# Slot dependences by quarter, a separate conversion clock, second V buffers and a halo prefetch in a hybrid decoder layer

## Chip, cores, metric

One Trainium2 chip, all 8 cores. Each core computes half of one of four sequences (2048 own tokens; the second half also needs keys and values of the first). The metric is the device time of the slowest core in microseconds. Most executions agree within 0.3%; in some, the cores of one die show a lower granted clock (TensorE's clock as the profile gives it, as a share of the full one) and the time is some per cent longer ("slow state").

## The reference, cut to what matters

```python
h = rmsnorm(x, norm_mix_pre)                       # x: (4, 4096, 2048)
q, k, v, u, g_attn, g_pool = split(h @ w_in)       # 1024, 1024, 1024, 1024, 2048, 2048
y_attn = stick_breaking_attention(q, k, v) @ w_attn_branch   # 8 heads of 128
y_pool = (pool(u) grouped @ w_pool_group * pool_scale) @ w_pool_branch
x = x + rmsnorm((sigmoid(g_attn)*y_attn + sigmoid(g_pool)*y_pool) @ w_out)
h = rmsnorm(x); up = causal_conv3(h @ w_up)        # 2 * 5632
x = x + rmsnorm((gelu(gate) * val) @ w_down)
x = x + rmsnorm(sigmoid(x @ w_ple_gate) * (p @ w_ple))
```

Stick-breaking weights telescope, so the kernel multiplies differences of neighbouring V rows: every V row is needed once more, shifted by one row.

## The kernel before

The program is recorded in Python: `P.op` and `P.dma` compare the regions that an instruction reads and writes with earlier ones and add semaphore waits. Timers (`after`) place later steps at a model time `now`, which advances with the recorded matmuls. A hold on a region fires timers early when a new instruction would collide with it (`guard`).

A core handles 8 chunks of 512 tokens: K and V for all, Q for the last four. From chunk 5 on this is interleaved on TensorE with attention(0), whose first part computes two halo tokens (extra tokens that the later three-tap convolution needs besides the core's own). Then come four mixers (U and pooling, gates, output projection), the first three beside attention(1) to (3), then the feed-forward and embedding parts. Weights come through eight slots of 512 KB. Mixer weights are first converted from float32 to bf16, DRAM to DRAM, two units at a time, by GpSimd's DMA queue.

```python
def mmq(pieces, reads, writes, start=True, q=4):       # 16 matmuls in quarters
    for a in range(0, n, q):
        ...
        P.op("pe", f, reads=reads, writes=writes)
        yield ...
# a token-major group (V of chunks 5..7, U, output projection): 4 slots, 4 blocks of tokens
rd = [s[1].r() for s in sl]                            # every quarter reads all four slots
for q_, ns in enumerate(mmq(pieces, rd + [hT[hb].r()], [bkr(b)])):
    if streamed and blk == 3:
        W.done(sl[q_][0])                              # frees the slot: refilled at once
    yield ns

def conv_every(ns):
    if conv:
        convert(conv[0], conv[0] + 2); conv.popleft()  # 1 MB written, 2 MB read
        after(ns, lambda: conv_every(ns))              # re-arms at now + ns

def t1():                                              # end of p0_v(c): the shifted V
    P.dma("sp", s_v[0], [(Vs[0:127], Vv[1:128]), (Vs[127:128, :, 0:3, :], Vv[0:1, :, 1:4, :]),
                         (Vs[127:128, :, 3, :], upv[0:1])], ...)
...
after(2000, t1, ...); after(11000, t2, ...)            # t2: subtraction on DVE
after(16500, t3, ...)                                  # t3: store of the differences

for h in range(NH):                                    # halo tokens in attention(0)
    kb_ = ldk(cc, h)                                   # load, used by the very next matmul
    P.op("pe", ... kb_ ...)
    yield 1500, 213
```

Of the kernel before, what the change touches and what calls it, by code (L numbers as in the profile page):

```python
# [216 lines left out]
def build_program():  # L217
# [23 lines left out]
    with contextlib.ExitStack() as es:  # L241
# [85 lines left out]
        off[0] = mix_lo  # L327
        wk = alloc(16 * 1024, BF16)
        assert off[0] <= mix_hi
        Vb = Buf(SBT, oT[1].lo, 4096, BF16)  # L330
        Vsh = Buf(SBT, G[1].lo, 4096, BF16)

        def bfm(i, j):
            return Buf(SBT, (hT[i % 2].lo, hT[i % 2].lo + 8192, oT[i % 2].lo, sga.lo)[j], D, F32)
# [11 lines left out]
        def bkr(b, n=1):  # L346
            return ("ps", b, b + n)
# [96 lines left out]

        def drain_all():
            drain()
            while timers:
                fire()

        def chain(entries, bufs=()):  # L450
# [5 lines left out]
        def dma_after(ns, q, sem, pairs, reads, writes):  # L456
            after(ns, lambda: P.dma(q, sem, pairs, reads=reads, writes=writes), reads, writes)

        def mmq(pieces, reads, writes, start=True, q=4):
            n = len(pieces)  # L460
            for a in range(0, n, q):
                sub = pieces[a:a + q]

                def f(e, sub=sub, a=a):
                    ins = None
                    for i, (o, l, r) in enumerate(sub):
                        ins = e.matmul(o, l, r, start=(start and a + i == 0), stop=(a + i == n - 1), skip_group_check=True)  # L467
                    return ins
                P.op("pe", f, reads=reads, writes=writes)
                yield sum(p[2].shape[-1] for p in sub) / 2.4  # L470

        def mm_now(pieces, reads, writes, start=True):
# [62 lines left out]
            P.dma("pool", s_cv, [(ws[u0:u1].rearrange("n p c -> (n p) c"), wst[u0:u1].rearrange("n p c -> (n p) c"))],  # L535
                  writes=[("ws", u0, u1)])

        def conv_every(ns):
            if conv:
                convert(conv[0], conv[0] + 2)  # L540
                conv.popleft()
                after(ns, lambda: conv_every(ns))

        def conv_all(u):
            while conv and conv[0] <= u:
# [136 lines left out]
                    yield ns  # L682
                kq_out(b, KS[c, h], ("ks", c * 8 + h, c * 8 + h + 1))

        Vv = Vb.v().rearrange("p (h b d) -> p h b d", h=NH, b=4)
        Vs = Vsh.v().rearrange("p (h b d) -> p h b d", h=NH, b=4)
        upv = uprev.v().rearrange("p (h d) -> p h d", d=128)

        def p0_v(c, streamed):
            hb = c % 2  # L690
            hv = hTv[hb]
            for cg in range(2):
                if streamed:
                    sl = [W.take(U_V + cg * 4 + ku) for ku in range(4)]
                for blk in range(4):
                    b = nb()
                    if streamed:
                        pieces = [(bank(b), hv[:, k, blk * 128:(blk + 1) * 128], sl[k // 4][1].k3(512)[:, k % 4, :]) for k in range(16)]
                        rd = [s[1].r() for s in sl]
                    else:  # L700
                        pieces = [(bank(b), hv[:, k, blk * 128:(blk + 1) * 128], wv3[:, cg * 16 + k, :]) for k in range(16)]
                        rd = [wv.r(cg * 8192, (cg + 1) * 8192)]
                    for q_, ns in enumerate(mmq(pieces, rd + [hT[hb].r()], [bkr(b)])):
                        if streamed and blk == 3:
                            W.done(sl[q_][0])
                        yield ns
                    evac(Vv[:, cg * 4:cg * 4 + 4, blk, :], bank(b).rearrange("p (h d) -> p h d", d=128), [bkr(b)], [Vb.r()])
            vr, vsr_, ur = Vb.r(), Vsh.r(), uprev.r()
            dvreg = ("dvs", c * 8, c * 8 + 8)

            def t1():
                P.dma("sp", s_v[0], [(Vs[0:127], Vv[1:128]), (Vs[127:128, :, 0:3, :], Vv[0:1, :, 1:4, :]),
                                     (Vs[127:128, :, 3, :], upv[0:1])], reads=[vr, ur], writes=[vsr_])
                if c >= 3:
                    P.dma("sp", s_v[2], [(VS[c - 3].rearrange("h p x -> p h x"), Vb.v().rearrange("p (h x) -> p h x", h=NH))],
                          reads=[vr], writes=[("vs", c - 3, c - 2)])

            def t2():
                for hh in range(2):
                    P.op("dve", lambda e, hh=hh: e.tensor_tensor(  # L720
                        out=Vsh.v(hh * 2048, (hh + 1) * 2048), in0=Vsh.v(hh * 2048, (hh + 1) * 2048),
                        in1=Vb.v(hh * 2048, (hh + 1) * 2048), op=ALU.subtract), reads=[vsr_, vr], writes=[vsr_])

            def t3():
                P.dma("sp", s_v[3], [(DVS[c].rearrange("h p x -> p h x"), Vsh.v().rearrange("p (h x) -> p h x", h=NH))],
                      reads=[vsr_], writes=[dvreg])
                P.dma("sp", s_v[1], [(upv[0:1], Vv[0:1, :, 0, :])], reads=[vr], writes=[ur])
            vsd = [("vs", c - 3, c - 2)] if c >= 3 else []
            after(2000, t1, [vr, ur], [vsr_] + vsd)
            after(11000, t2, [vr], [vsr_])  # L730
            after(16500, t3, [vr], [vsr_, ur, dvreg])
# [21 lines left out]
        def attention(t, pos0=0):  # L753
# [21 lines left out]
            if t == 0:  # L775
                yield 20000, 0
                prev = None
                for cc in range(3, -1, -1):
                    b = ZB[zb[0] % 2]
                    zb[0] += 1  # L780
                    for h in range(NH):
                        kb_ = ldk(cc, h)
                        P.op("pe", lambda e, kb_=kb_, h=h, b=b: e.matmul(bank(b), qh.v(h * 128, (h + 1) * 128), kb_.v(), start=(h == 0),
                                                                     stop=(h == 7), skip_group_check=True),
                             reads=[kb_.r(), qh.r()], writes=[bkr(b)])
                        yield 1500, 213
                    gb = gr.next()
                    P.op("act", lambda e, gb=gb, b=b: e.activation(out=gb.v(), in_=bank(b), func=AF.Sigmoid, scale=-QSCALE),
                         reads=[bkr(b)], writes=[gb.r()])
# [18 lines left out]
                    evac(asb.v(), at[:, 0:NT], [bkr(ab)], [asb.r()], eng="act")  # L808
                    yield 2000, 0
                    for h in range(NH):  # L810
                        dv = lddv(cc, h)
                        rd = [dv.r(), asb.r()]
                        pcs = [(bank(OB, 2, 2 * h), dv.v(kb * 128, (kb + 1) * 128), asb.v(kb * 128 + 2 * h, kb * 128 + 2 * h + 2))
                               for kb in range(4)]
                        if cc == 3:
                            vv = ldv(3, h)
                            pcs.append((bank(OB, 2, 2 * h), vv.v(0, 128), idz.v(0, 2)))
                            rd += [vv.r(), idz.r()]

                        def f(e, pcs=pcs, first=(cc == 3 and h == 0)):  # L820
                            ins = None
                            for i, (o_, l, r) in enumerate(pcs):
                                ins = e.matmul(o_, l, r, start=(first and i == 0), stop=False, skip_group_check=True)
                            return ins
                        P.op("pe", f, reads=rd, writes=[bkr(OB)])
                        yield 1500, 250
                evac(o.k3(NTH)[:, :, NT:NTH], bank(OB, 16).rearrange("p (h t) -> p h t", t=2), [bkr(OB)], [o.r()], eng="dve")

            groups = [(h, cc) for h in range(NH) for cc in range(c, -1, -1)]
# [127 lines left out]
        def att_total(t):  # L957
            c = 4 + t
            n = NH * (c * 4 * 640 + (10 * 128 * 3 + 512) / 2.4) + 4000
            if t == 0:  # L960
                n += 20000 + 4 * (8 * 1500 + 7000 + 8 * 1500)
            return n

        def mixer(i):
            hb = i % 2
# [2 lines left out]
            pcs_cols = [(0, 257), (257, 514)] if i == 0 else [(0, 512)]  # L968
            wcol = NTH if i == 0 else NT

            def load_h(j):
                P.dma("sp", s_hT[j % 2], [(hTv[j % 2][:, :, 0:NT], H1[j].rearrange("p (k t) -> p k t", t=NT))],
                      reads=[("h1", j, j + 1)], writes=[hT[j % 2].r()])
            if i == 0:
                load_h(0)
                ctx = Buf(SBT, XN[0].lo, 2048, BF16)
                P.dma("sp", s_st[2], [(ctx.v(), HC)], reads=[("hc", 0, 1)], writes=[ctx.r()])
                P.op("dve", lambda e: e.tensor_copy(hv[:, :, NT:NTH], h2c.v().rearrange("p (k t) -> p k t", t=2)),
                     reads=[h2c.r()], writes=[hT[hb].r()])
            for cg in range(2):  # L980
                sl = [W.take(U_U + cg * 4 + ku) for ku in range(4)]
                for blk in ([4] if i == 0 else []) + [0, 1, 2, 3]:
                    b = nb()
                    if blk == 4:
                        lhs = lambda k: ctx.k3(128)[:, k, :]
# [4 lines left out]
                        rd = [hT[hb].r()]  # L990
                        dst, dr = ub.v(blk * 1024 + cg * 512, blk * 1024 + cg * 512 + 512), ub.r(blk * 1024, (blk + 1) * 1024)
                    pieces = [(bank(b), lhs(k), sl[k // 4][1].k3(512)[:, k % 4, :]) for k in range(16)]
                    for q_, ns in enumerate(mmq(pieces, rd + [s[1].r() for s in sl], [bkr(b)])):
                        if blk == 3:
                            W.done(sl[q_][0])
                        yield ns
# [85 lines left out]
            for cg in range(4):  # L1082
                sl = [W.take(U_O + cg * 4 + ku) for ku in range(4)]
                blks = [0, 1, 2, 3] + ([4] if i == 0 else [])
                for blk in blks:
# [3 lines left out]
                    ob = bank(b) if blk < 4 else PS[0:2, b * 512:b * 512 + 512]  # L1089
                    pieces = [(ob, mxT.v(k * NTH + c0, k * NTH + c0 + m), sl[k // 4][1].k3(512)[:, k % 4, :]) for k in range(16)]  # L1090
                    lastb = blk == blks[-1]
                    for q_, ns in enumerate(mmq(pieces, [s[1].r() for s in sl] + [mxT.r()], [bkr(b)])):
                        if lastb:
                            W.done(sl[q_][0])
                        yield ns
# [113 lines left out]
        front(1)  # L1209
        run(p0_k(0))  # L1210
        drain()
        conv_every(11500)
        run(p0_k(1))
        run(p0_v(0, False))
        front(2)
# [13 lines left out]
        def p0b():  # L1229
            for c in range(5, 8):  # L1230
                drain()
                p0_begin(c)
                if c < 7:
                    front(c + 1)
                for x_ in phase(p0_k(c), p0_v(c, True), p0_q(c)):
                    yield x_
        stats.append(run(p0b(), attention(0), 72 * GRP, att_total(0)))
# [445 lines left out]
```

## Time and profile before

| | us |
|---|---|
| median of 20 runs (lowest, highest) | 5706.8 (5692.4, 6051.1) |
| profiled run, slowest core | 5689.3 |
| first work of the feed-forward part | 3494.5 |
| PE busy, share of the span | 4498.0, 79% |

The slices show where to look: each digit is PE's busy share, or the granted clock, of a fortieth of the span, in tenths.

```profile
PE   5201676458679978977997786999999999999988
...
PEclk9655888679889989988998897999999999999999
```

The second to fourth slices are the hole; slices 5 to 11 are the chunks and the halo tokens; the dips at 15, 18 and 19, 22 and 23, and 25 are output projections; from slice 26 on PE is full. Two more lines belong to each chunk's shift. The first is from the timeline of the SyncE queue (start, duration of the issues), the second from the chain that ended last.

```profile
674.84 19.74 SPq L202 DMA_DIRECT2D SB<-SB  x3
```

```profile
693.30 24.43 DMA SB<-SB
```

Issuing the shift's three transfers holds the SyncE queue 20 us, and the data lands 24 us later. All else that SyncE loads stands behind it: the next issue in the timeline is at 694.73 us. From 706 to 716 us only its packets move: 32 of 8 KB, one after another, 0.31 us each, 26 GB/s and 6.3% of the 16 DMA engines' time.

The same trace shows what the clock costs. In the first output projection, at a clock of 0.83, the three groups of four matmuls between refill waits that the prediction prints took 1.02, 1.86 and 1.87 us: the second and third 0.84 and 0.85 us longer than the first, besides the waits themselves.

### The profile page before, as it was taken

The numbers are of one execution on the slowest core, as the hardware profiler recorded it, in microseconds if no ns is written. First come the engines' busy times: TensorE is split into PE (matmuls) and PEld (weight loads), VectorE is DVE, ScalarE is ACT, GpSimd is POOL, SyncE is SP. The second block draws the span as 40 slices with busy tenths as digits, with TensorE's granted clock in tenths as the row PEclk, the third lists the DMA queues.
The fourth block names the chain that finished last, engine by engine and source line by source line (L and its number), as shares of the span: only waits on it lengthen the run. The fifth ranks groups of instructions, "written<-read, shape, count | busy, mean of one in ns | idle before, by whom it ended". The sixth has DMA issues, their size and how long they took to land.

```text
span 5689.3 us, 73576 instructions; the slowest of 8 cores (5664.5 to 5689.3 us)
## 1 busy us (share of the span) xinstructions
PE 4498.0 (79%) x25664; PEld 2331.5 (41%) x25664; DVE 2278.7 (40%) x2149; ACT 1846.1 (32%) x3066; POOL 284.5 (5%) x652
## 2 busy tenths in 40 slices
PE   5201676458679978977997786999999999999988
PEld 2000332124348534533553333666644444444434
DVE  2000221017547647855884313444411444431154
ACT  2000111016445536644663212333300233320134
POOL 1000000000000000000000001111100111100000
PEclk9655888679889989988998897999999999999999
DMA  9898244334334334434443436777756644446653
GB/s 192 101 113 114 87 140 134 107 100 126 111 124 139 124 106 155 140 109 139 148 141 114 161 126 132 139 127 128 127 173 212 152 78 77 76 107 198 200 204 113
DMA packets 292013, 752.95 MB, mean 132 GB/s; under 512 B 61386, under 2 KB 174474, under 8 KB 270602
## 3 DMA queue, kind: packets, MB, share of 16 engines
q1 hardware_dynamic: 259156, 566.54, 30.3%
q0 software_dynamic: 32496, 181.72, 21.6%
q8 instruction: 213, 3.49, 0.3%
q14 instruction: 148, 1.21, 0.1%
HBM read 827.59 MB, written 171.44 MB: 176 GB/s over the span
## 4 chain that ended last, share of the span: by engine, by line
PE 69%; DMA 14%; another core or an unknown queue 7%; SPq 4%; DVE 3%; issue 2%; ACT 1%; POOL 0%; DVEq 0%; ACTq 0%; POOLq 0%
PE PS L467 30%; PE PS L1302 20%; PE PS L1353 9%; DMA SB<-ws 5%; SPq L202 4%; PE PS L914 3%; PE PS L881 3%; PE PS L843 3%; DMA SB<-SB 1%; DMA KS<-SB 1%; DMA SB<-KS 1%; DMA SB<-X 1%; DMA SB<-DVS 1%; DMA SB<-xr 1%
## 5 line engine op out<-in xcount | busy, mean ns | idle before, releaser
L467 PE MATMUL PS<-SB 128*128 128x512 bf16 (+2 forms) x9656 | 2141.0, 370 | 399.8 <-DMA SB<-ws 264.3
L467 PEld LDWEIGHTS PS<-SB 128*128 128x128 bf16 x9656 | 905.5, 100 | 1268.0 <-issue 576.0
L1302 PE MATMUL PS<-SB 128*128 128x342 bf16 (+1 forms) x7040 | 1228.5, 337 | 7.3 <-ACT SB L1319 7.3
L486 ACT ACTIVATE SB<-PS 128x512 bf16<-128x512 bf16 (+4 forms) x1017 | 608.7, 604 | 1716.7 <-PE PS L881 475.3
L771 DVE TENSOR_TENSOR_SCAN SB<-SB 128x512 bf16<-128x512 f32 (+1 forms) x836 | 975.4, 1201 | 217.4 <-ACT SB L854 187.4
L1302 PEld LDWEIGHTS PS<-SB 128*128 128x128 bf16 x7040 | 683.0, 97 | 551.9 <-issue 11.8
L1353 PE MATMUL PS<-SB 128*128 128x512 bf16 x2816 | 613.4, 381 | 12.6 <-DMA SB<-ws 12.5
L568 ACT ACTIVATE SB<-SB 128x512 bf16<-128x512 f32 (+3 forms) x245 | 216.7, 885 | 968.8 <-DVE SB L490 785.8
L490 DVE COPY SB<-PS 128x512 f32<-128x512 f32 (+3 forms) x197 | 135.2, 687 | 965.4 <-PE PS L1353 441.0
L589 PE MATMUL PS<-SB 128*128 128x128 bf16 x1024 | 81.2, 243 | 549.9 <-DVE SB L574 530.7
L854 ACT ACTIVATE SB<-PS 128x512 f32<-128x512 f32 (+1 forms) x832 | 476.6, 573 | 34.5 <-PE PS L843 19.0
L1326 DVE SCALAR_TENSOR_TENSOR SB<-SB 128x1024 f32<-128x1024 f32 x176 | 226.1, 1285 | 614.9 <-ACT SB L1319 614.9
L1353 PEld LDWEIGHTS PS<-SB 128*128 128x128 bf16 x2816 | 275.9, 98 | 348.0 <-issue 20.3
L1316 ACT ACTIVATE SB<-PS 128x1026 f32<-128x1026 f32 (+1 forms) x176 | 180.2, 1024 | 686.9 <-PE PS L1302 675.8
L914 PE MATMUL PS<-SB 128*128 128x512 bf16 (+1 forms) x960 | 322.4, 358 | 40.7 <-DMA SB<-DVS 35.6
L490 DVE CAST SB<-PS 128x512 bf16<-128x512 f32 (+2 forms) x151 | 97.9, 652 | 611.4 <-PE PS L467 404.0
L881 PEld LDWEIGHTS PS<-SB 128*128 128x128 bf16 x3136 | 249.9, 100 | 187.4 <-issue 28.8
L843 PE MATMUL PS<-SB 128*128 128x512 bf16 (+1 forms) x832 | 313.2, 377 | 14.7 <-ACT SB L854 12.9
L881 PE MATMUL PS<-SB 128*128 128x128 bf16 x3136 | 321.6, 224 | 2.3 <-ACT SB L486 1.1
L589 PEld LDWEIGHTS PS<-SB 128*128 128x128 bf16 x1024 | 73.6, 110 | 567.9 <-issue 557.7
L574 DVE SCALAR_TENSOR_TENSOR SB<-SB 128x2048 f32<-128x2048 f32 (+2 forms) x98 | 229.8, 2345 | 116.3 <-POOL SB L563 100.0
L1329 DVE SCALAR_TENSOR_TENSOR SB<-SB 128x1024 f32<-128x1024 f32 x176 | 226.1, 1285 | 18.4
(53 smaller groups left out, 1460.7 us busy)
## 6 DMA issues: line engine op xcount, KB each, us to landing
SB<-ws SPq DMA_DIRECT2D x520, 512.0 KB, 3.5
SB<-wst POOLq DMA_DIRECT2D x192, 512.0 KB, 6.2
ws<-wst POOLq DMA_DIRECT2D x74, 1024.0 KB, 42.0
SB<-xr SPq DMA_DIRECT2D x48, 1024.0 KB, 7.9
SB<-X SPq DMA_DIRECT2D x36, 1024.0 KB, 9.1
X<-SB SPq DMA_DIRECT2D x32, 1024.0 KB, 7.3
SB<-KS SPq DMA_DIRECT2D x240, 128.0 KB, 2.8
SB<-DVS SPq DMA_DIRECT2D x240, 128.0 KB, 3.0
```

The costliest lines, as they stand in the source:

```text
L202: e.dma_start(out=o, in_=i).then_inc(h, 16)
L467: ins = e.matmul(o, l, r, start=(start and a + i == 0), stop=(a + i == n - 1), skip_group_check=True)
L486: P.op("act", lambda e: e.activation(out=dst, in_=src, func=AF.Copy), reads=reads, writes=writes)
L490: P.op("dve", lambda e: e.tensor_copy(dst, src), reads=reads, writes=writes)
L574: P.op("dve", lambda e: e.scalar_tensor_tensor(out=dst, in0=xv, scalar=cv, in1=gv, op0=ALU.mult, op1=ALU.mult), reads=[xr_, small.r(col, c ...
L771: P.op("dve", lambda e: e.tensor_tensor_scan(out=pb.v(lo, NT), data0=gb.v(lo, NT), data1=mask, initial=init, op0=ALU.mult, op1=ALU.max), r ...
L843: P.op("pe", lambda e: e.matmul(bank(bk, NT - lo, lo), q_.v(b_ * 128, (b_ + 1) * 128), kb_.v(lo, NT), start=True, stop=True), reads=[kb_.r ...
L854: P.op("act", lambda e: e.activation(out=gb.v(lo, NT), in_=bank(bk, NT - lo, lo), func=AF.Sigmoid, scale=-QSCALE), reads=[bkr(bk)], writes ...
L881: ins = e.transpose(at[:, q_ * 128:(q_ + 1) * 128], src[q_].v(kb * 128, (kb + 1) * 128), ident)
L914: ins = e.matmul(o_, l, r, start=(first and i == 0), stop=False, skip_group_check=True)
L1302: ins = e.matmul(bank(bs[bi], c1 - c0), w3[:, k, :], hT2v[:, k, c0:c1], start=(k == 0), stop=(k == 15), skip_group_check=True)
L1353: ins = e.matmul(bank(b), actb[kk].v(q_ * 512 + blk * 128, q_ * 512 + (blk + 1) * 128), w3[:, k, :], start=(kk == 0), stop=(kk == NF - 1), ...
```

## The change

Intent: remove waits of TensorE before the feed-forward part by (1) letting each quarter of a token-major group depend on its own slot, (2) re-arming the conversion timer from its own scheduled time, 13 us apart, and not draining it with the other timers, (3) giving chunk 1's V buffers of its own in weight slots not yet in use, (4) loading halo keys and values two ahead, (5) loading the first mixer's inputs during chunk 7. The diff, cut to its core:

```diff
-            while timers:
+            while any(t[2] is not None for t in timers):
                 fire()
...
-        def mmq(pieces, reads, writes, start=True, q=4):
+        def mmq(pieces, reads, writes, start=True, q=4, rq=None):
...
-                P.op("pe", f, reads=reads, writes=writes)
+                P.op("pe", f, reads=reads + ([rq[a // q]] if rq else []), writes=writes)
...
-        def conv_every(ns):
+        def conv_every(ns, t=None):
+            t = now[0] if t is None else t
             if conv:
                 convert(conv[0], conv[0] + 2)
                 conv.popleft()
-                after(ns, lambda: conv_every(ns))
+                after(t + ns - now[0], lambda: conv_every(ns, t + ns))
...
+            Vb, Vsh = (Vb0, Vsh0) if c != 1 else (Buf(SBT, ringb[0].lo, 4096, BF16), Buf(SBT, ringb[2].lo, 4096, BF16))
...
+                for _ in range(2):
+                    more_k()
+                    more_v()
...
-                        kb_ = ldk(cc, h)
+                        kb_ = kl.popleft()
                         P.op("pe", ...)
-                        yield 1500, 213
+                        more_k()
+                        yield 2000, 213
... (the same for differences and values)
-                    for q_, ns in enumerate(mmq(pieces, [s[1].r() for s in sl] + [mxT.r()], [bkr(b)])):
+                    for q_, ns in enumerate(mmq(pieces, [mxT.r()], [bkr(b)], rq=[s[1].r() for s in sl])):
... (the same for V and U; in U the halo block moves from first to fourth)
-        conv_every(11500)
+        conv_every(13000)
...
+                else:
+                    mixer_first_loads()
```

More of the change, by code (lines that the diff above doesn't have):

```diff
@@ L329, in build_program @@
         assert off[0] <= mix_hi
-        Vb = Buf(SBT, oT[1].lo, 4096, BF16)
-        Vsh = Buf(SBT, G[1].lo, 4096, BF16)
+        Vb0 = Buf(SBT, oT[1].lo, 4096, BF16)
+        Vsh0 = Buf(SBT, G[1].lo, 4096, BF16)
         def bfm(i, j):
@@ L683, in p0_k @@
                 kq_out(b, KS[c, h], ("ks", c * 8 + h, c * 8 + h + 1))
-        Vv = Vb.v().rearrange("p (h b d) -> p h b d", h=NH, b=4)
-        Vs = Vsh.v().rearrange("p (h b d) -> p h b d", h=NH, b=4)
         upv = uprev.v().rearrange("p (h d) -> p h d", d=128)
@@ L690, in p0_v @@
             hb = c % 2
+            Vb, Vsh = (Vb0, Vsh0) if c != 1 else (Buf(SBT, ringb[0].lo, 4096, BF16), Buf(SBT, ringb[2].lo, 4096, BF16))
+            Vv = Vb.v().rearrange("p (h b d) -> p h b d", h=NH, b=4)
+            Vs = Vsh.v().rearrange("p (h b d) -> p h b d", h=NH, b=4)
             hv = hTv[hb]
@@ L698, in p0_v @@
                         pieces = [(bank(b), hv[:, k, blk * 128:(blk + 1) * 128], sl[k // 4][1].k3(512)[:, k % 4, :]) for k in range(16)]
-                        rd = [s[1].r() for s in sl]
+                        rd = []
                     else:
@@ L702, in p0_v @@
                         rd = [wv.r(cg * 8192, (cg + 1) * 8192)]
-                    for q_, ns in enumerate(mmq(pieces, rd + [hT[hb].r()], [bkr(b)])):
+                    for q_, ns in enumerate(mmq(pieces, rd + [hT[hb].r()], [bkr(b)], rq=[s[1].r() for s in sl] if streamed else None)):
                         if streamed and blk == 3:
@@ L777, in attention, with more_k, more_v @@
                 prev = None
+                kq = deque((cc, h) for cc in range(3, -1, -1) for h in range(NH))
+                vq = deque(kq)
+                kl, vl, sl_ = deque(), deque(), deque()
+                def more_k():
+                    if kq:
+                        kl.append(ldk(*kq.popleft()))
+                def more_v():
+                    if vq:
+                        cc_, h_ = vq.popleft()
+                        if cc_ == 3:
+                            sl_.append(ldv(3, h_))
+                        vl.append(lddv(cc_, h_))
+                for _ in range(2):
+                    more_k()
+                    more_v()
+                yield 4000, 0
                 for cc in range(3, -1, -1):
@@ L810, in attention @@
                     for h in range(NH):
-                        dv = lddv(cc, h)
+                        dv = vl.popleft()
                         rd = [dv.r(), asb.r()]
@@ L815, in attention @@
                         if cc == 3:
-                            vv = ldv(3, h)
+                            vv = sl_.popleft()
                             pcs.append((bank(OB, 2, 2 * h), vv.v(0, 128), idz.v(0, 2)))
@@ L825, in attention @@
                         P.op("pe", f, reads=rd, writes=[bkr(OB)])
-                        yield 1500, 250
+                        more_v()
+                        yield 2000, 250
                 evac(o.k3(NTH)[:, :, NT:NTH], bank(OB, 16).rearrange("p (h t) -> p h t", t=2), [bkr(OB)], [o.r()], eng="dve")
@@ L960, in att_total, with load_h, mixer_first_loads @@
             if t == 0:
-                n += 20000 + 4 * (8 * 1500 + 7000 + 8 * 1500)
+                n += 24000 + 4 * (8 * 2000 + 7000 + 8 * 2000)
             return n
+        def load_h(j):
+            P.dma("sp", s_hT[j % 2], [(hTv[j % 2][:, :, 0:NT], H1[j].rearrange("p (k t) -> p k t", t=NT))],
+                  reads=[("h1", j, j + 1)], writes=[hT[j % 2].r()])
+        ctx = Buf(SBT, XN[0].lo, 2048, BF16)
+        def mixer_first_loads():
+            load_h(0)
+            P.dma("sp", s_st[2], [(ctx.v(), HC)], reads=[("hc", 0, 1)], writes=[ctx.r()])
         def mixer(i):
@@ L969, in mixer @@
             wcol = NTH if i == 0 else NT
-            def load_h(j):
-                P.dma("sp", s_hT[j % 2], [(hTv[j % 2][:, :, 0:NT], H1[j].rearrange("p (k t) -> p k t", t=NT))],
-                      reads=[("h1", j, j + 1)], writes=[hT[j % 2].r()])
             if i == 0:
-                load_h(0)
-                ctx = Buf(SBT, XN[0].lo, 2048, BF16)
-                P.dma("sp", s_st[2], [(ctx.v(), HC)], reads=[("hc", 0, 1)], writes=[ctx.r()])
                 P.op("dve", lambda e: e.tensor_copy(hv[:, :, NT:NTH], h2c.v().rearrange("p (k t) -> p k t", t=2)),
@@ L981, in mixer @@
                 sl = [W.take(U_U + cg * 4 + ku) for ku in range(4)]
-                for blk in ([4] if i == 0 else []) + [0, 1, 2, 3]:
+                for blk in ([0, 1, 2, 4, 3] if i == 0 else [0, 1, 2, 3]):
                     b = nb()
@@ L992, in mixer @@
                     pieces = [(bank(b), lhs(k), sl[k // 4][1].k3(512)[:, k % 4, :]) for k in range(16)]
-                    for q_, ns in enumerate(mmq(pieces, rd + [s[1].r() for s in sl], [bkr(b)])):
+                    for q_, ns in enumerate(mmq(pieces, rd, [bkr(b)], rq=[s[1].r() for s in sl])):
                         if blk == 3:
```

## The prediction

> **What bounds the kernel now.** I took the page, then the busy table by stretches, the chain that ended last, the waits, and last the timelines of the worst stretches. The busy table comes first because one average (PE 79% of 5689 us) hides very different stages. Its columns are stretch, length, then busy us (instructions) of PE, PE weight load, DVE, ACT, POOL, then granted clock, DMA share, GB/s.
>
> ```profile
> 172.00:548.00 376.00, 10.18 (x48) 4.41 (x45) 2.68 (x3) 0.00 (x0) 18.43 (x38) 0.52 0.97 112
> 548.00:900.00 352.00, 236.92 (x1325) 116.03 (x1326) 76.56 (x75) 63.57 (x79) 11.06 (x30) 0.83 0.31 108
> 900.00:1300.00 400.00, 211.44 (x982) 87.53 (x981) 45.11 (x44) 41.13 (x56) 7.12 (x16) 0.72 0.36 116
> 1300.00:1600.00 300.00, 232.26 (x1499) 122.04 (x1500) 198.29 (x191) 167.62 (x337) 0.00 (x0) 0.89 0.40 128
> 1670.00:1940.00 270.00, 265.64 (x2379) 209.59 (x2380) 189.38 (x236) 157.65 (x344) 0.00 (x0) 1.00 0.45 148
> 1940.00:2160.00 220.00, 159.33 (x841) 72.26 (x840) 100.87 (x97) 80.82 (x170) 4.39 (x6) 0.83 0.29 96
> 3500.00:5690.00 2190.00, 2111.67 (x11306) 1090.42 (x11303) 835.51 (x699) 663.42 (x806) 185.68 (x458) 0.98 0.60 142
> ```
>
> From 3500 us on (feed-forward and embedding) PE works 96% of the time, and the change touches nothing there. Everything to be had lies in the first 3500 us. There are three kinds of loss: a hole of 376 us with PE and DVE empty and DMA full; the projection and first-attention stages (548 to 1600 us), where PE works 65%; and the output projections (1940 to 2160 us and three more such), where PE works 72% at a clock of 0.83.
>
> What the hole is, from the chain, the waits and the timeline of GpSimd and of the SyncE queue:
>
> ```profile
> 171.82 373.24 another core or an unknown queue
> ...
> DVE SB L720 <- DMA SB<-SB: 515.9, 5, 373.4
> ...
> 171.22 3.98 POOL L202 DMA_DIRECT2D ws<-wst  x8
> 171.90 206.56 SPq L202 DMA_DIRECT2D SB<-SB  x3
> 184.95 0.49 POOL L202 DMA_DIRECT2D ws<-wst  x1 [9.75 <-DMA ws<-wst]
> ```
>
> GpSimd issues one weight conversion (float32 to bf16, DRAM to DRAM) after another, eight in flight and one finishing every 9.4 us, for 39 in a row. The one-row shift of chunk 0's V (SB<-SB) lies among them and takes 373 us; the subtraction on DVE waits for it, and all else behind DVE. The source says why 39 come at once. Chunk 1's V goes into chunk 0's buffer, so the recorder fires timers until the shift's timers (up to 16.5 us ahead) are done. The conversion timer re-arms at "now + 11.5 us", now stands still, and so it fires until no conversion is left.
>
> The other two losses, from the waits and PE's timeline:
>
> ```profile
> PE PS L467 <- DMA SB<-ws: 264.3, 79, 25.1
> PE PS L783 <- DMA SB<-KS: 75.6, 13, 36.7
> PE PS L823 <- DMA SB<-DVS: 63.8, 9, 37.3
> ...
> 1949.76 1.02 PE L467 MATMUL PS<-SB 128*2 128x512 bf16 x4 [2.58 <-DMA SB<-ws]
> 1954.51 1.86 PE L467 MATMUL PS<-SB 128*2 128x512 bf16 x4 [3.73 <-DMA SB<-ws]
> 1959.90 1.87 PE L467 MATMUL PS<-SB 128*2 128x512 bf16 x4 [2.13 <-DMA SB<-ws]
> ```
>
> Four matmuls, a wait, four, a wait, four, a wait: in the last block of every token-major group, quarter 0 frees its slot, the slot is refilled at once, and quarter 1, declared as a reader of all four slots, waits for that refill, which holds data it never reads. The code has three such waits in each of 6 V, 8 U and 16 output groups, 90; the trace shows 79. One of 25.1 us is of another kind (the SyncE queue was held up), so the false ones are about 78 and 239 us, 3.1 us each.
>
> [...] The shift moves 127 rows: alone it took 24 us (24.43, 25.32 and 24.11 in the chain), where a 1 MB load of x took 5.6 us. [...] conversion packets carry 32 KB and take 4.5 us, the shift's 8 KB packets 0.32 us, and between 180 and 360 us the SyncE queue moved 2.6 GB/s; between 110 and 140 us, with five conversions in flight, it moved 27 GB/s where it moves 110 without. So conversions beat everything SyncE loads. [...]
>
> **The change, part by part.**
>
> *1. Per-quarter slots.* Each quarter now waits for its own slot. In the mixer stages the refill waits are 53.3 (1940 to 2160), 55.5 (2460 to 2680), 64.9 less 25.1 (2980 to 3170) and 36.9 (3170 to 3500), plus about 20 in the U part of the first mixer: 205 us. Clock: columns through the array at 2.4 GHz make 127.8, 127.1, 100.6 and 238.1 us in these stretches (matmul counts by shape times columns), against PE busy of 159.3, 154.6, 123.4 and 262.0: 106 us lost to the slow clock. I credit two thirds of it, as a few other waits stay: 70. Sum **-275**. Another 34 us of refill waits lie in the V groups of chunks 5 to 7.
>
> *2. The hole.* 373 us go. Chunk 0's subtraction will still wait for its shift on DVE as the four others did ((515.9 - 373.4) / 4 = 36): **-337**.
>
> *3. What the conversions cost elsewhere.* All 39 still run, 9.4 us each, 367 us of full DMA. In the built program's order of GpSimd's instructions they stand one at a time between the norm's small operations (19 of them), then as two bursts of 4, and as a burst of 12 after the last norm of chunk 7's front. (The first five, together at 96 us, are as before.) A burst goes out as fast as eight semaphores allow, so the 12 are another flood of 113 us, in the middle of a stage that lives on SyncE's loads. At 27 GB/s against its usual 110 to 130, PE soon starves: eight weight slots are 27 us of matmuls, two halo keys 4 us. I take 85 us for the burst of 12, 25 for each burst of 4, 3 for each single (57): **+192**, half of the 367. This is the softest number here.
>
> *4. Halo prefetch.* Waits for halo keys, differences and values: 75.6 + 63.8 + 10.1, of which 36.7 and 37.3 are two that lie behind a shift. The other 75 us are 23 waits of 3.3 us, and loads issued two ahead (two steps of about 1.8 us of other matmuls each) cover most of such a latency. With 25 us of clock: **-85**, some left for loads caught by a conversion.
>
> *5. First loads of the mixer.* The wait for HC, 11.7 us, goes: **-12**. With the 34 us of part 1 that makes -131 before 1600 us besides the hole.
>
> Second V buffers for chunk 1 remove the flushing of timers; their worth is inside part 2. Matmuls, evictions and bytes are unchanged.
>
> Sum: -275 - 337 + 192 - 85 - 12 - 34 = -551, so 5689 - 551 = 5138; I round to **5125**, as a smaller clock loss should also show between 548 and 1600 us (PE busy there 681 us, columns 586).
>
> **Rivals.**
>
> *A. The conversions take the hole back.* If DMA is the real bound up to 1600 us, spreading them hides little: +330 in place of +192 gives about 5270. For: the 27 GB/s, the burst of 12, and 41 us for one key store at 108 us with five in flight. Against: DMA share without them is only 0.31 to 0.40.
>
> *B. They hide almost wholly,* about +60: 5000. For: PE stalls there anyway for each shift, some 40 us a chunk. Against: the shift is on the same DMA engines and is lengthened by each of them.
>
> *C. The false wait was covering a true one.* If slots cannot be refilled in time, half of the 275 stays: about 5260. A group needs 2 MB in 13.7 us (64 matmuls at 213 ns), 154 GB/s, in the last mixer alone, and less where attention is between. Against: 237 GB/s was moved at 4300 to 4400 us, and the next group's slots are already full.
>
> *D. DVE or ACT becomes the bound in the mixers.* Against: at 1670 to 1940 us, with PE full, DVE is at 70%, ACT at 58%.
>
> **Range and chances.** Part 1 is counted twice (waits and columns) and safe within 50 us; parts 2 and 3 together decide, between -280 and 0 about. That gives 5000 to 5270 in the fast state; as runs of before spread upward in the slow state, I take 4980 to 5270. Even rival A and C together leave some 5% gain: faster 0.97, same 0.02, slower 0.01.
>
> **What would show it.** Right: no stretch over 60 us without PE work; refill waits of L467 under 60 us in all; clock 0.95 or more and PE over 90% busy in the output projections; conversions spread up to about 1100 us, in a trail with a dense burst near its end, PE thin within that burst. The stage from 3500 us takes 2190 us as before, only earlier. Wrong: refill waits of the same number with other releasers (C); the stretch from 172 us to the first mixer shorter by under 200 us (A) or by over 480 (B). I would also be wrong if the 12 conversions did not slow SyncE's loads.

## The result

The changed kernel takes 5184.0 us in the median of 10 runs (5165.7 to 5557.9; four of them in the slow state) against 5706.8 of before. The ratio is 0.9077, interval 0.9056 to 0.9098. Ratios here are the mean time of one kernel's fast runs over that of the other's in the same rounds, so they are not quite the ratio of the medians. The prediction was 5125, range 4980 to 5270.

The clearest reading comes from markers in the two traces of fast runs: times of one instruction, on the slowest core. "V differences n" is the subtraction of chunk n; "gates" are the first and last gate sigmoids of a mixer.

| marker or stretch | before | after | difference |
|---|---|---|---|
| V differences 0, at | 545.2 | 231.3 | -313.9 |
| V differences 0 to 4 | 351.4 | 406.6 | +55.2 |
| V differences 4 to 7 | 631.5 | 676.6 | +45.1 |
| V differences 7 to end of first U part | 141.9 | 109.4 | -32.5 |
| gates of mixers 0, 1, 2, 3 (first to last) | 236.5, 261.0, 267.9, 161.5 | 236.2, 260.7, 267.9, 161.5 | 0 |
| last gate to the end of the next mixer's U part (after mixer 3: to the feed-forward part) | 245.2, 236.1, 236.8, 130.1 | 170.1, 163.2, 169.8, 65.0 | -280.1 |
| first feed-forward matmul to the end | 2194.8 | 2194.8 | 0 |

The gate stretches and the last 2195 us are identical, as they should be: the change does nothing there. The gain is 246 us before the first mixer's gates and 280 us in the output projections and U parts.

The busy table of after, for the former hole, a new gap, the first and the third output projection, and the rest (columns as in the prediction):

```profile
172.00:548.00 376.00, 197.24 (x1000) 95.56 (x998) 68.20 (x63) 54.55 (x66) 17.05 (x41) 0.75 0.53 124
...
944.00:1046.00 102.00, 0.27 (x2) 0.14 (x2) 0.00 (x0) 0.00 (x0) 1.48 (x3) 0.51 0.96 129
...
1690.00:1840.00 150.00, 138.68 (x877) 69.07 (x875) 104.59 (x101) 84.72 (x181) 4.39 (x6) 1.00 0.44 146
...
2566.00:2736.00 170.00, 136.75 (x856) 71.03 (x854) 103.50 (x100) 82.58 (x168) 2.96 (x8) 0.92 0.58 173
...
2972.00:5167.00 2195.00, 2117.21 (x11333) 1094.02 (x11330) 838.20 (x701) 664.87 (x808) 190.88 (x464) 0.98 0.60 143
```

In the 376 us where PE had 10 us of work it now has 197. The first output projection works 92% of the time at full clock (72% at 0.83 before); the second and fourth are like it (90% and 91%), but the third stays at 80% and 0.92, with one wait of 22.9 us for DVE (L590 for L575). And there is a gap of 102 us that was not there. The waits (total, times, longest) and the timeline around 930 us name it:

```profile
DVE SB L722 <- DMA SB<-SB: 288.4, 6, 64.3
...
PE PS L803 <- DMA SB<-KS: 151.9, 5, 101.7
...
PE PS L844 <- DMA SB<-DVS: 86.2, 8, 38.2
...
PE PS L467 <- DMA SB<-ws: 3.9, 4, 1.8
```

```profile
925.37 4.00 POOL L202 DMA_DIRECT2D ws<-wst  x8
...
938.04 115.80 SPq L202 DMA_DIRECT2D SB<-KS  x6
...
938.56 0.49 POOL L202 DMA_DIRECT2D ws<-wst  x1 [9.20 <-DMA ws<-wst]
...
1045.81 0.59 PE L803 MATMUL PS<-SB 128*128 128x512 bf16 x1 [101.73 <-DMA SB<-KS]
```

The refill waits of L467 fell from 264.3 us to 3.9. The gap is the burst of 12 conversions: eight issued at 925 us, four more as each finishes, and a halo key loaded two ahead, but behind them, arrives 102 us late. The waits for halo keys and differences (L803, L844) became fewer, 13 for 22 before, but not shorter in all: 238 us for 139 before.

### The profile page after: what moved, and what is told of

Its sections match the earlier page's. It is cut to its first block, busy times and chain, and to the rows that moved or that the text cites. A ratio compares the mean times of both kernels' runs of the same rounds, so it can differ in the third digit from the quotient of the medians.

```text
span 5167.3 us, 73593 instructions; the slowest of 8 cores (5143.3 to 5167.3 us)
## 1 busy us (share of the span) xinstructions
PE 4392.0 (85%) x25664; PEld 2311.6 (45%) x25664; DVE 2274.1 (44%) x2149; ACT 1846.5 (36%) x3066; POOL 287.8 (6%) x652
## 4 chain that ended last, share of the span: by engine, by line
PE 72%; DMA 12%; SPq 7%; DVE 3%; issue 2%; another core or an unknown queue 2%; ACT 2%; POOL 0%; DVEq 0%; ACTq 0%; POOLq 0%
PE PS L467 29%; PE PS L1329 22%; PE PS L1380 10%; SPq L202 7%; PE PS L936 3%; PE PS L903 3%; PE PS L865 3%; DMA KS<-SB 3%; DMA SB<-DVS 2%; DMA SB<-SB 1%; DMA SB<-KS 1%; DMA SB<-X 1%; DMA SB<-xr 1%; DVE SB L575 1%
## 5 line engine op out<-in xcount | busy, mean ns | idle before, releaser
L467 PE MATMUL PS<-SB 128*128 128x512 bf16 (+2 forms) x9656 | 2057.9, 361 | 145.8 <-DVE SB L490 98.3
L467 PEld LDWEIGHTS PS<-SB 128*128 128x128 bf16 x9656 | 895.3, 99 | 959.1 <-issue 226.8
L486 ACT ACTIVATE SB<-PS 128x512 bf16<-128x512 bf16 (+3 forms) x1017 | 609.6, 605 | 1378.3 <-PE PS L467 546.5
L1329 PEld LDWEIGHTS PS<-SB 128*128 128x128 bf16 x7040 | 682.7, 97 | 554.4 <-issue 12.5
L1380 PEld LDWEIGHTS PS<-SB 128*128 128x128 bf16 x2816 | 276.1, 98 | 348.3 <-issue 21.1
L936 PE MATMUL PS<-SB 128*128 128x512 bf16 (+1 forms) x960 | 313.1, 348 | 44.5 <-DMA SB<-DVS 38.3
L590 PE MATMUL PS<-SB 128*128 128x128 bf16 x1024 | 84.4, 248 | 285.6 <-DVE SB L575 269.5
L865 PE MATMUL PS<-SB 128*128 128x512 bf16 (+1 forms) x832 | 307.3, 371 | 18.7 <-ACT SB L876 13.6
L903 PEld LDWEIGHTS PS<-SB 128*128 128x128 bf16 x3136 | 242.6, 98 | 177.6 <-issue 13.4
L575 DVE SCALAR_TENSOR_TENSOR SB<-SB 128x2048 f32<-128x2048 f32 (+2 forms) x98 | 229.7, 2344 | 109.3 <-POOL SB L564 92.9
L1346 ACT ACTIVATE SB<-PS,SB 128x1026 f32<-128x1026 f32 (+1 forms) x176 | 212.4, 1207 | 36.9 <-DMA X<-SB 20.1
```

The source lines that it names most:

```text
L467: ins = e.matmul(o, l, r, start=(start and a + i == 0), stop=(a + i == n - 1), skip_group_check=True)
L486: P.op("act", lambda e: e.activation(out=dst, in_=src, func=AF.Copy), reads=reads, writes=writes)
L575: P.op("dve", lambda e: e.scalar_tensor_tensor(out=dst, in0=xv, scalar=cv, in1=gv, op0=ALU.mult, op1=ALU.mult), reads=[xr_, small.r(col, c ...
L865: P.op("pe", lambda e: e.matmul(bank(bk, NT - lo, lo), q_.v(b_ * 128, (b_ + 1) * 128), kb_.v(lo, NT), start=True, stop=True), reads=[kb_.r ...
L903: ins = e.transpose(at[:, q_ * 128:(q_ + 1) * 128], src[q_].v(kb * 128, (kb + 1) * 128), ident)
L936: ins = e.matmul(o_, l, r, start=(first and i == 0), stop=False, skip_group_check=True)
```

## The experiments

All comparisons with the changed kernel are the difference of the two ratios to before, times 5700 us (before's fast time), unless a trace is named.

| label | edit | median us | ratio to before | against the changed kernel, us |
|---|---|---|---|---|
| e1_allslots | slot dependences as before | 5536.1 | 0.9735 | +375 |
| e2_bothold | old timer and one V buffer | 5274.0 | 0.9248 | +97 |
| e3_noconv | 39 conversions left out | 4932.9 | 0.8677 | -228 |
| e4_halolate | halo loads at use | 5288.8 | 0.9265 | +107 |
| e5_paced | conversions tied to PE's progress | 5094.7 | 0.8934 | -82 |
| e6_split | shift in 112 and 15 rows | 5002.5 (half slow) | 0.8595 | -275 |
| e7_before_split | the same cut on the kernel before | 5451.4 | 0.9553 | (-255 against before) |
| e8_split_paced | both | 4832.6 | 0.8472 | -345 |
| e9_vshared | one V buffer, new timer | 5178.8 | 0.9083 | +3 |
| e10_clockold | old timer, two V buffers | 5184.1 | 0.9089 | +7 |

All but e3_noconv gave correct results.

### Slot dependences undone

```diff
-                P.op("pe", f, reads=reads + ([rq[a // q]] if rq else []), writes=writes)
+                P.op("pe", f, reads=reads + (list(rq) if rq else []), writes=writes)
```

> The changed kernel, but each quarter of a token-major group is again declared a reader of all four slots. Theory (the refill waits were false, and each cost its 3.1 us and some slow clock): the four stretches from the last gate of one mixer to the first of the next work go back from 170, 163, 170 and 65 us to about 245, 236, 237 and 130 us, refill waits of L467 to about 240 us in 78, time up by 280 to 315 us against the changed kernel (about 5460). Rival (the gain in these stretches came from other parts, or the waits were covering true ones): up by less than 150 us.

Measured: up by 375 us (355 between the profiled runs; the interval of the ratio is wide here, 0.9678 to 0.9791), more than expected, and so are the refill waits, 400 us in place of 240. The four stretches are 243.6, 233.2, 236.6 and 133.4 us, 278.7 more than in the changed kernel, as expected. One wait line of this run and one stretch of the busy table, an output projection:

```profile
PE PS L467 <- DMA SB<-ws: 400.1, 84, 57.3
```

```profile
1753.00:1997.00 244.00, 178.42 (x979) 84.67 (x998) 120.03 (x123) 94.25 (x200) 4.39 (x6) 0.85 0.32 109
```

The count of waits is about that of before (84, there 79), with the clock back at 0.85. That the next group's slots were full all along is shown by the changed kernel's 3.9 us. Another 81 us fall before the first gates: 59 in chunks 5 to 7 and 26 in the first U part, less 4 gained before. The refill waits there are 195 us, 54 in the kernel before. The two longest, 57.3 and 35.9 us, lie among the 12 conversions, here issued from 941 to 985 us; the wait of 101.7 us for a halo key is not there (the longest is 38.5), so in part this is the same loss at another instruction. The parts are not independent.

### Both guards against the row of conversions undone

```diff
-                after(t + ns - now[0], lambda: conv_every(ns, t + ns))
+                after(ns, lambda: conv_every(ns))
...
-            Vb, Vsh = (Vb0, Vsh0) if c != 1 else (...)
+            Vb, Vsh = (Vb0, Vsh0) if c != 99 else (...)
```

> The changed kernel with the old conversion timer and one V buffer, both at once; the built order shows 39 conversions in a row again. Theory (the hole was worth 337 us and about 190 to 240 us of it came back as delays elsewhere): hole of about 370 us at 172 us, no gap from conversions later, time up by 95 to 145 us against the changed kernel. Rival A (all of it came back elsewhere): up by less than 40. Rival B (hidden almost wholly): up by over 270.

Measured: up by 97 us, in the theory's range. The hole is back, in one wait of 373 us:

```profile
PE PS L590 <- DVE SB L575: 557.4, 17, 373.0
```

After it the chunks run as in the kernel before: V differences 0 to 4 take 351.4 us, the same to a tenth. The hole is worth little net, since without it the conversions slow what follows (by 245 us, next run).

### The conversions left out

```diff
+                if conv[0] < 18 or conv[0] >= U_D:
                     convert(conv[0], conv[0] + 2)
...
+                        w_ = 8 + u % 8 if u < U_UP else u
-                        P.dma("sp", s_ring[s], [(ringb[s].v(), ws[u])], ...)
+                        P.dma("sp", s_ring[s], [(ringb[s].v(), ws[w_])], ...)
```

> Wrong result on purpose: the 39 conversions of mixer weights after the first five are left out, and those weight loads read the ten units that were converted, so that all other instructions and transfers stay. It measures what the spread conversions still cost. Theory: 190 to 250 us less than the changed kernel (4915 to 4975), with the gap of 102 us near 945 us gone. Rival A: over 330 us less. Rival B: under 80 us less.

Measured: 228 us less by the ratios (this interval is wide too, 0.8620 to 0.8734). In the traces the end of the first U part comes at 1178.6 us in place of 1423.9, 245 us earlier; the parts after it are unchanged within 12 us. By chunk, from the markers, what the conversions cost ("single" is one that is not issued in a burst):

| V differences | conversions within, about | changed | without | cost us |
|---|---|---|---|---|
| start to 1 | 3, besides the first five | 299.6 | 280.8 | 19 |
| 1 to 2 | 5 single | 114.8 | 93.4 | 21 |
| 2 to 3 | 4 single | 116.7 | 90.4 | 26 |
| 3 to 4 | 1 and a burst of 4 | 106.8 | 87.5 | 19 |
| 4 to 5 | 3 and a burst of 4 | 200.7 | 149.7 | 51 |
| 5 to 6 | 3 and the burst of 12 | 265.3 | 149.8 | 115 |
| 6 to the first U part | 0 | 320.0 | 327.1 | -7 |

Against e2_bothold, where the same 39 stand in one row, this kernel reaches the end of the first U part 344.6 us earlier. That is what the hole was worth, and 245 of it came back.

### Halo loads at their use

```diff
-                for _ in range(2):
-                    more_k()
-                    more_v()
...
+                        more_k()
                         kb_ = kl.popleft()
                         P.op("pe", ...)
-                        more_k()
                         yield 2000, 213
```

> The changed kernel with the halo keys, differences and values loaded at the matmul that uses them, as before the change, all else kept (also the new time shares). Theory: the 23 short waits of 3.3 us come back, with some slow clock, up by 60 to 100 us. Rival (the loads now wait behind shifts and conversions anyway, so that prefetching two ahead is worth little): up by less than 30 us.

Measured: up by 107 us (103 between the traces, before the first gates), slightly above the range. There are 31 waits in the two lines below (13 in the changed kernel, 22 in the kernel before), and those for differences are longer than in the kernel before (63.8 us in 9), since here they meet conversions (the two longest, 64.2 and 47.6 us, lie between 989 and 1105 us, and the 12 were issued from 986 to 1026):

```profile
PE PS L842 <- DMA SB<-DVS: 235.5, 17, 64.2
PE PS L801 <- DMA SB<-KS: 82.5, 14, 38.0
```

### Conversions tied to TensorE's progress

```diff
-        def convert(u0, u1):
+        def convert(u0, u1, pe=None):
             P.dma("pool", s_cv, [...],
-                  writes=[("ws", u0, u1)])
+                  writes=[("ws", u0, u1)], after=pe)
...
-                convert(conv[0], conv[0] + 2)
+                convert(conv[0], conv[0] + 2, ("pe", esems["pe"], P.cnt["pe"]))
```

> The changed kernel, but each conversion also waits on TensorE's count at the point where it was recorded, so that bursts of 4 and 12 cannot form. Same conversions, same order. Theory (much of the 251 us that the conversions still cost is the burst: the chunk with the 12 took 115 us longer than without conversions): no gap over 60 us near chunk 7, 60 to 100 us less than the changed kernel (about 5100). Rival (only the volume on the DMA engines counts, however it is spread): within 30 us of the changed kernel.

Measured: 82 us less. The last 12 conversions now go out one by one between 901 and 1167 us. The chunk that held the burst takes 183.8 us in place of 265.3, the next one 253.9 in place of 210.6. The same stretch of time shows PE thin, its longest gap 47.1 us:

```profile
900.00:950.00 50.00, 29.12 (x147) 13.12 (x145) 4.05 (x5) 4.50 (x7) 1.08 (x2) 0.82 0.59 142
950.00:1000.00 50.00, 9.45 (x53) 4.11 (x54) 3.14 (x3) 0.60 (x1) 0.49 (x1) 0.60 0.42 128
1000.00:1050.00 50.00, 34.62 (x171) 15.76 (x167) 25.89 (x25) 19.61 (x39) 0.98 (x2) 0.80 0.86 232
1050.00:1100.00 50.00, 43.05 (x289) 23.71 (x290) 37.82 (x37) 33.66 (x69) 1.47 (x3) 0.93 0.60 142
```

So a quarter to a third of the conversions' 245 us lay in their clustering, which the rival (volume alone) denies. (A quarter, because the edit also spreads the first five, which e3_noconv leaves as they are: V differences 0 comes 15 us earlier here.)

### The shift cut into 112 and 15 rows

```diff
-                P.dma("sp", s_v[0], [(Vs[0:127], Vv[1:128]), (Vs[127:128, ...
+                P.dma("sp", s_v[0], [(Vs[0:112], Vv[1:113]), (Vs[112:127], Vv[113:128]), (Vs[127:128, ...
```

> The changed kernel with the shift of V cut from 127 rows into 112 and 15[...]. Theory ([...] the shift takes 24 us and the SyncE queue stalls 17 us on its issue, eight times): shift landed within about 10 us where no conversion is in flight, chunk periods down from 91 towards 65 us, 150 to 280 us less than the changed kernel (4900 to 5030). Rival (the shift is slow because of its place in the queue, or the wait is set by something else): under 50 us less.

> The kernel before with only the same cut of the shift; its 39 conversions still go out in one row. It asks what made the hole so long: [...] the shift, served one packet per 3 us among conversion packets, or the flood as such. Theory [...] the first subtraction comes within about 60 us of the shift's issue in place of 373 us, PE has work during the flood, though thin; with the other shifts 250 to 400 us less than before (5300 to 5450). Rival flood: PE stays idle through most of the 370 us since every load starves; only the later shifts gain, 100 to 200 us less (5500 to 5600).

On the changed kernel: 275 us less. (Its profiled run fell in the slow state; what is read here is core 2, on the undisturbed die.) Where conversions come singly, the chunk period falls: V differences 1 to 2 take 66.2 us in place of 114.8, 2 to 3 92.5 in place of 116.7. The wait for the burst of 12 stays as it was, 104.7 us.

On the kernel before, the cut tells two things apart. This is its SyncE queue and its busy table in the hole:

```profile
170.89 3.10 SPq L202 DMA_DIRECT2D SB<-SB  x4
...
224.99 253.33 SPq L202 DMA_DIRECT2D SB<-xr  x2
```

```profile
250.00:300.00 50.00, 0.00 (x0) 0.00 (x0) 0.00 (x0) 0.00 (x0) 2.46 (x5) 0.50 0.99 112
...
400.00:450.00 50.00, 3.34 (x8) 1.05 (x8) 1.67 (x3) 3.19 (x4) 2.46 (x5) 0.50 0.98 115
```

The shift is issued in 3 us in place of 207, and the first subtraction comes at 220 us, 49 us after the issue. The theory is right that the cut makes the shift fast (the traces do not record the engine of a packet, so why it does is not shown). It is wrong about the hole: PE is empty again from 250 to 400 us and nearly so to 450, because the next loads of x starve instead (the queue needs 253 us to issue two). The subtraction of chunk 1 comes at 562.8 us (before: 624.7), so only 62 us of the hole went. The other gain comes after the flood: the periods of chunks 2, 3 and 4 are 58.4, 62.9 and 54.5 us, before 93.2, 91.8 and 86.9, and the subtraction of chunk 2 starts 7.5 us after the issue of its shift, 43 us before the cut. The total, 255 us less, lies at the edge of the first expectation, but mostly by the way that the rival named; the rival's size (100 to 200) was too small.

### Both together

> Both the cut shift and the paced conversions on the changed kernel, as a version that should beat both kernels: 200 to 360 us less than the changed kernel (4810 to 4970), less than either alone. If the two hide behind each other (a burst falls into a shift's stall), the sum is less than the two gains added.

Measured: ratio 0.8472 (0.8453 to 0.8491), 4832.6 us in the median, 345 us less than the changed kernel and the best of all. The gains add (82 and 275 against 345), so neither hides behind the other.

### Which of the two guards was needed

> The changed kernel with chunk 1's V in chunk 0's buffers again, the conversion timer as changed. The built order of GpSimd's instructions is the changed kernel's: one by one, 4, 4 and 12. Theory (the clock alone prevents the row of 39; the buffers only spare chunk 1 a wait for chunk 0's stores): no hole over 80 us near 172 us, 10 to 40 us more than the changed kernel. Rival (the buffers are needed as well): 80 us or more.

> The changed kernel with the old conversion timer (re-armed at the standing now), but chunk 1's own V buffers kept. The built order has no row of 39: singles, pairs, 4, 4 and 13. Theory (the row needs both, a forced flush and a timer that re-arms at a standing clock; either one gone is enough): within 25 us of the changed kernel. Rival (the clock is what does it): 60 us or more above it.

Each edit is one half of e2_bothold's. Measured: +3 and +7 us, both within the interval of the changed kernel. Either guard alone prevents the row of 39, as the built order of GpSimd's instructions had shown. The second V buffers save nothing measurable beyond that; the 10 to 40 us that I had expected of them are not there.

## Why the prediction was right, and where it was off

The direction, the size and the places were right: 523 us between medians, 551 in its sum. By its own steps:

1. **Per-quarter slots, -275 and -34.** Right. The four stretches, 255 of the 275, gave -280.1. Undoing it alone costs another 81 us before the first gates, more than the 54 (34 and 20 of the first U part) I had counted, as refills meet conversions there. Where they do not, the count holds: e2_bothold has the row of conversions of the kernel before, and its V differences 4 to 7 take 512.2 us in place of 631.5, 119 less as in my sum (34 + 85 of the halo), and from there to the end of the first U part it takes 31 us less (20 + 12 in my sum).
2. **The hole, -337.** Right: 344.6 us between e2_bothold and e3_noconv. My reason for its length was only half right. I said that the subtraction on DVE waits for the shift and all else behind it. With a fast shift (e7_before_split) the hole stays for the most part, because SyncE's loads starve among the conversions (253 us to issue two loads of x).
3. **What the conversions cost elsewhere, +192.** The mechanism was right (the burst of 12 near chunk 7 is there, with a 102 us gap where I had taken 85), the size too small: 245 us. The term "3 for each single" failed: in the two chunks that hold only singles, nine of them cost 47 us, 5 each. The chunk with the 12 and three singles cost 115, where my terms give 94, and the chunk with one burst of 4 and three singles 51 for 34. These 53 us and the 13 of point 6, less some 25 us that the output projections gave beyond my sum and 8 of the hole, are most of the 42 us between 5125 and the 5167 of the profiled run.
4. **Halo prefetch, -85.** Right where no conversion is in flight, by the 119 us under 1. In the changed kernel undoing it costs 103 to 107, but what it saves there is a loss that the conversions enlarge: halo waits are 238 us with it, 318 without and 139 in the kernel before.
5. **First loads of the mixer, -12.** About 6, if one takes it from the stretch before the first gates (141.9 before, 135.7 with the slot dependences undone); no run isolates it.
6. **The rounding from 5138 to 5125** for clock loss between 548 and 1600 us went the wrong way. No such extra gain showed: from the V differences of chunk 0 to those of chunk 7 the time grew by 100 us.

Of the rivals, A (the conversions take the hole back) was closest: seven tenths came back. B and C fell: e3_noconv shows that the hiding is poor, and 3.9 us of refill waits show that no true wait stood behind the false ones. D fell too, as the gate stretches are unchanged and PE is full in them.

Two of my signs for being right did not come: a stretch of 102 us without PE work (I allowed 60, though my own 85 us for the burst spoke against that), and the third output projection, with PE at 80% and a clock of 0.92 (I asked for 90% and 0.95).

What stays open: why singles cost 5 us each. One packet of a conversion takes about as long (4.5 us in the kernel before, 108 to 140 us), but no run varied the packet size, so a link is not shown. Nor does a run isolate the spacing of 13 us, the larger time shares of the halo steps, the timers no longer drained, or the moved halo block of U.

## What to carry to other kernels

Declare what each instruction really reads: a slot that is freed and refilled inside a group turns a too-wide read into a wait for data of the next group, at the price of a full load and a slower clock (here refill waits of 264.3 us for 3.9, and a clock of 0.83 for 1.00 in the first output projection). A bulk transfer that is nobody's bottleneck can still stop a stage that lives on small loads, as the 12 conversions did here for 102 us; tie its issue to the progress of the work, not to a planned time, and look for bursts where the issuing engine has nothing else to wait for. When removing a large hole, ask first where its transfers will go: here seven tenths of 345 us came back.

## What the traces show of queues and clock

- The packets of two queues can be very unequal. In the kernel before, a DRAM-to-DRAM conversion's packets held 32 KB and took 4.5 us (108 to 140 us), those of the shift and of the loads of x 8 KB and 0.31 to 0.32 us. SyncE's queue moved 103 GB/s from 598 to 650 us and 116 from 30 to 60 us, without conversions; it moved 27 from 110 to 140 us, with five conversions in flight, and 2.6 from 180 to 360 us, with only the shift in it beside the row.
- The shift of 127 rows takes 24 us for 1 MB, where a 1 MB load of x took 5.6 us (median from 548 to 900 us). Issuing it also holds the issuing queue: 18.7 to 22.9 us for three transfers alone, 207 us beside the row of conversions, 3.1 and 2.9 us for four transfers once cut into 112 and 15 rows (e7_before_split).
- In the fast state eight cores with dense matmuls stayed at 1.00: from 4200 to 4300 us of the kernel before, 465 matmuls of 512 columns in 100 us, 2.38 GHz (456 or more on every core). In the slow state, core 5 of e6_split showed 0.81 with PE full, at 382 in 100 us, 1.96 GHz. Over the whole run cores 4 to 7 had 0.912 to 0.917 there, cores 0 to 3 0.954 to 0.958. The two busy-table lines, first of the kernel before, then of e6_split on its slow die:

```profile
4200.00:4300.00 100.00, 100.00 (x465) 45.36 (x464) 8.36 (x13) 7.99 (x23) 0.00 (x0) 1.00 0.45 153
```

```profile
4500.00:4600.00 100.00, 100.00 (x382) 41.44 (x381) 24.37 (x20) 5.78 (x16) 2.96 (x8) 0.81 0.60 201
```
